# Second memory attention: keys and values made during the mix and kept in DRAM; the mix's last two products grouped around a late operand

## The chip, the cores and the metric

One Trainium2 chip, one of its cores. The core has five engines that run side by side, each with a queue of its own: PE (TensorE, matrix products into PSUM), DVE (VectorE), ACT (ScalarE), POOL (GpSimd) and SP (SyncE, which issues all the DMAs here). The metric is the time of one execution of the kernel on the device, in microseconds (us), as the median of several runs.

## The reference, cut to what matters

The program is two transformer models in a row on one sequence of 512 tokens of width 1024. The first has two layers (attention mixers, a memory attention and a feed-forward part in each). The second has one layer, and the change is in that one:

```python
p_rw, p_s5, p_gla, p_gate = split(rms_norm(x, norm_mix) @ w_in)
y_rw, y_s5, y_gla = rwkv7_mix(p_rw), s5_mix(p_s5), gla_mix(p_gla)       # 512 wide each
g = sigmoid(p_gate)                                                      # three gates, 1024 wide
x = x + (g[0]*(y_rw @ w_branch[0]) + g[1]*(y_s5 @ w_branch[1]) + g[2]*(y_gla @ w_branch[2])) @ w_out
q = rms_norm(x, norm_xattn) @ wq                                         # 4 heads of 256
k, v = split(rms_norm(mem, norm_mem) @ wkv)                              # 256 memory rows; needs no x
x = x + softmax(q @ k.T / 16) @ v @ wo
x = x + conv_ffn(rms_norm(x, norm_ffn))
```

The keys and values depend on the memory alone, which is an input. All is computed in fp32: each operand of a product is split into a high and a low half, and a product is three matmuls (high by high, high by low, low by high).

## The kernel before

Activations lie transposed, as tiles of 128 features by 512 tokens. A weight comes in from DRAM as a raw tile of 128x512 (`wraw`, 7 buffers, 256 KB); ACT copies the high half (`wh`, L312) and DVE subtracts for the low half (`wl`, L314), 5 buffers each. `proj_g` takes one block of 128 output features at a time: one PSUM bank, 8 or 4 operands deep, three matmuls each (L282 to L284), then `emit`, which takes the bank's content out. `proj_late` works on up to three chunks of 256 output features at once, with two banks for each (two of kind `mm`, two `ch`, two `si`; there are 3, 3 and 2 of them). It multiplies all operands but the last for all six banks, then asks for the last one and finishes the banks in order. In the kernel before only the first model's memory attention uses it.

The order is planned while the program is written. `kit.push` queues a generator as filler: `kind` 0 and 1 are two queues of product work that take turns, kind 2 are small steps with due times. `kit.fill(us)` runs filler for so many planned microseconds, `kit.need` runs a job to its end, and `kit.flush` runs all that is left. A scheduler then orders each engine's instructions by its own estimate of when they are ready and when a tile is free; on the chip each engine works off that list in order. Working tiles (128x512) come from rings `a`, `b`, `c`. A job's `stream` (its kind plus one, unless given) says by `kit.room` which ring it draws on: in the mix stream 0 is `a` (22 tiles), 1 is `b` (11), 2 and 3 are `c` (21).

The mix (`mix`, L2229) pushes S5 and after it GLA as kind 1; as kind 0 the low-rank part of RWKV and the gates 1 (`gates_g`, L2193). When S5 is done, merging branch 1 (`merge_g`, L2206) and gates 2 are pushed; when GLA is done, merging branch 2 and gates 0. RWKV itself (`rwkv`, L1709) runs in the foreground with fills between its steps: two pairs of `rwkv_a` steps, the inverse (`rwkv_invert`, L1487, on DVE, L1506 and L1507, while filler runs), and four `rwkv_b`, for head pairs 2, 3, 0, 1 in this order. Each `rwkv_b` ends with a norm (L468 on POOL, spread by L498 and L510), a bonus add on POOL (L1700) and a split. After that `merge_g(0)` runs: each block is multiplied by its gate on DVE (L2215), added to the sum of the other branches on POOL (L2217) and split again (L248, L245). Then `w_out` runs block by block with the memory's norm (`memory`, L2260: loads L188, splits L263 and L264, squares L2277 and adds L2278) as filler between. `add` (L1338) adds a block to x and `normed` splits it for the next products. The memory attention (`cross`, L2286) makes keys and values of head 0 and query 0, then pushes query, keys and values of heads 1 to 3 as filler for the score steps, 4.5 planned us at each.

Of the kernel before, what the change touches and what calls it, by code (L numbers as in the profile page):

```python
# [10 lines left out]
F32 = mybir.dt.float32  # L11
# [6 lines left out]
S = 512  # L18
D = 1024
DT = D // 128  # L20
MEM = 256
# [14 lines left out]
BOTH = {"mm": "mm ch si", "si": "si", "ch": "ch"}  # L36
X_BOTH = {"mm": "mm ch", "si": "si", "ch": "mm ch"}
LATE = {"mm": "mm", "si": "si", "ch": "ch", "tr": "ch"}, dict(mm=3, ch=3, si=2)
SFLOW = "accc"
AB_FILL, CD_FILL, X_FILL = (0.9, 1.2), (1.15, 1.3, 1.1), (1.1, 1.4)  # L40


# [1198 lines left out]
def layouts2(mem_2, norm_mix_2, w_in_2, rw_mu_2, rw_w0_2, rw_w_up_2, rw_a0_2, rw_a_up_2, rw_g_up_2, rw_k_k_2,  # L1241
# [20 lines left out]
    up[:16, 0] = gla_gk_up_2[0]  # L1262
    o["gk_up"] = up
    o["w_gate"] = tiled(gate)
    o["w_br"] = np.stack([tiled(z) for z in w_branch_2[0]])
    o["w_out"] = tiled(w_out_2[0])
    o["w_glu"] = tiled(s5_w_glu_2[0])
    o["mem2T"] = np.ascontiguousarray(mem_2[0].T.reshape(4, 2, 128, MEM).transpose(0, 2, 1, 3)).reshape(4, 128, 2 * MEM)
    o["xa_wq"] = tiled(xa_wq_2[0])
# [50 lines left out]
class Second:  # L1320
# [885 lines left out]
    def merge_g(self, b, ys, job):  # L2206

        kit, nc, I = self.kit, self.nc, self.I
        kit.need(job)
        sig = self.gates[b]  # L2210

        def branch(m, p):
            s = sig[m]
            if m in self.merged:
                nc.vector.tensor_tensor(s, p, s, op=ALU.mult)  # L2215
                s, z = self.merged[m], s
                nc.gpsimd.tensor_tensor(s, s, z, op=ALU.add)  # L2217
            else:
                z, s = s, kit.keep("x")
                self.merged[m] = s  # L2220
                nc.vector.tensor_tensor(s, p, z, op=ALU.mult)
            if b == 0:
                self.O.append(kit.u())
                kit.split(s, *self.O[m])

        for c in range(4):
            yield from kit.proj_g(I["w_br"][b, c], [hl for hl, _ in ys], lambda i, p: branch(2 * c + i, p))

    def mix(self):  # L2229
        kit, I = self.kit, self.I  # L2230
        self.xs = kit.xs
        self.merged, self.gates, self.O = {}, {}, []
        gla, s5 = [], []

        def branch1():
            yield from self.s5_g(s5, lambda: kit.push(branch2(), kind=1))
            kit.push(self.merge_g(1, s5, g1))
            self.g2 = kit.push(self.gates_g(2))

        def branch2():  # L2240
            yield from self.gla_g(gla)
            kit.push(self.merge_g(2, gla, self.g2))
            self.g0 = kit.push(self.gates_g(0))

        kit.push(branch1(), kind=1)
        lora = kit.push(self.rwkv_lora())
        g1 = kit.push(self.gates_g(1))
        kit.fill(20.0)
        kit.need(lora)
        rw = self.rwkv()  # L2250
        kit.flush()
        kit.run(self.merge_g(0, rw, self.g0))
        job = kit.push(self.memory(), kind=2, stream=1)
        for c in range(4):
            kit.fill(3, 10)
            kit.run(kit.proj_g(I["w_out"][c], self.O, lambda i, p: self.add(2 * c + i, p, "norm_xattn")))
        kit.need(job)


    def memory(self):  # L2260

        kit, nc, I = self.kit, self.nc, self.I
        ms = self.ms = []
        mems = [kit.load("", src=src) for src in I["mem2T"]]
        yield -6
        for m in range(DT):
            if m % 2 == 0:
                mem, hl = mems[m // 2], kit.u()
            c = slice(m % 2 * MEM, m % 2 * MEM + MEM)
            ms.append([z[:, c] for z in hl])  # L2270
            kit.split_scaled(mem[:, c], self.vec("norm_mem", m), *ms[m])
            if m == 0:
                acc = kit.f(MEM)
                nc.scalar.square(acc, mem[:, c])
            else:
                sq = kit.f(MEM)
                nc.scalar.square(sq, mem[:, c])  # L2277
                nc.gpsimd.tensor_tensor(acc, acc, sq, op=ALU.add)  # L2278
            yield -1
        self.mr = kit.t([128, 2], "mr2", 1)  # L2280
        nc.vector.tensor_copy(self.mr, kit.rpow(kit.sums(acc, kit.ones, [tok(0), tok(1)]), 1.0 / D, EPS))
        big = kit.spread_begin(self.mr, 2)
        yield -4
        self.mrb = kit.spread_end(big)

    def cross(self):  # L2286
        kit, nc, I = self.kit, self.nc, self.I
        xs, ms, mr, mrb = kit.xs, self.ms, self.mr, self.mrb
        st, O = {}, {}
        sc = kit.small(4, "scq")  # L2290

        def keys(h):
            def emit(j, p):
                if not j:
                    hl = kit.u()
                    st["k", h] = [[z[:, j * MEM : j * MEM + MEM] for z in hl] for j in range(2)]
                f = kit.f(MEM)
                nc.vector.tensor_tensor(f, p, mrb, op=ALU.mult)
                kit.split(f, *st["k", h][j])

            yield from kit.proj_g(I["xa_wk"][h], ms, emit)

        def vals(h):
            st["v", h] = []

            def emit(b, p):
                st["v", h].append(kit.u(256))
                kit.split_scaled(p, mr[:, b : b + 1], *st["v", h][b])

            yield from kit.proj_tok_g(I["xa_wv"][h], ms, [tok(0), tok(1)], emit)  # L2310

        def query(h):
            st["q", h] = []
# [37 lines left out]

            return f

        kit.run(keys(0))
        kit.run(vals(0))
        kit.run(query(0))
        jobs = [[]] + [[kit.push(g(h)) for g in (query, keys, vals)] for h in range(1, 4)]

        def heads():
            for h in range(4):  # L2360
                kit.need(*jobs[h])
                qk = []
                for (qh, ql), (kh, kl) in zip(st["q", h], st["k", h]):
                    qk += [(qh, kh), (qh, kl), (ql, kh)]
                sums = kit.small(4, "sums")
                soft = kit.soft_full(sc, [sums[:, b : b + 1] for b in range(4)])
                yield Head(kit, qk, st["v", h], [(0, 256)] * 4, DENSE_K[:2], soft, done(h, sums), 4.5)

        kit.attention(heads())
        kit.flush()  # L2370
# [95 lines left out]
def program(tc, ctx, I, out):  # L2466
    kit = Kit(tc, ctx, I)
    f = First(kit)
    kit.banks(*APART)
    kit.room("abbb", a=26, b=31)  # L2470
    V, P = kit.nc.vector, kit.nc.gpsimd
    f.begin()
    kit.by(P)
    f.mixer_ab()
    kit.by(V)
    kit.share(X_BOTH)
    f.cross(0)
    kit.share(BOTH)
    kit.room("aaaa", a=50)
    f.ffn(0, f.g_mix[1])  # L2480
    kit.share(APART[0])
    kit.by(V, P)
    kit.room("abbb", a=24, b=33)
    f.mixer_cd()
    kit.by(V)
    kit.share(X_BOTH)
    f.cross(1)
    kit.banks(*LATE)
    kit.room("abbb", a=31, b=50-31)
    s = Second(kit)  # L2490
    take, done = handover(kit, f, s)
    job = kit.push(s.s5_make_g())
    f.ffn(1, take)
    kit.need(job)
    done()
    kit.room("abcc", a=22, b=11, c=54-22-11)
    s.reset = kit.load("reset")
    s.mix()
    kit.flow(SFLOW)
    s.cross()  # L2500
    kit.room("aaaa", a=50)
    s.ffn()
    s.finish(out)
# [13 lines left out]
```

## Time and profile before

| | before |
|---|---|
| median of 3 runs | 2703.43 us (2700.62 to 2705.85) |
| the profiled execution | 2697.67 us |
| its span, first to last instruction | 2695.9 us |
| PE busy | 2573.7 us (95%) |
| DVE busy | 1594.7 us (59%) |
| ACT busy | 1180.1 us (44%) |
| POOL busy | 518.9 us (19%) |
| DMA | 258.51 MB, 96 GB/s on the mean |
| granted TensorE clock, mean | 0.978 of full speed |

The mix of the second model runs from about 1441 us to 2153 us of the span (its last output products overlap with the keys of head 0), the memory attention until about 2327. Busy shares are of the whole span; what a stage is bound by has to be read in that stage. PE's matmuls overlap, so the durations printed for them are longer than the distance of their starts.

### The profile page before, as it was taken

The numbers are of one execution on the slowest core, as the hardware profiler recorded it, in microseconds if no ns is written. First come the engines' busy times: TensorE is split into PE (matmuls) and PEld (weight loads), VectorE is DVE, ScalarE is ACT, GpSimd is POOL, SyncE is SP. The second block draws the span as 40 slices with busy tenths as digits, with TensorE's granted clock in tenths as the row PEclk, the third lists the DMA queues.
The fourth block names the chain that finished last, engine by engine and source line by source line (L and its number), as shares of the span: only waits on it lengthen the run. The fifth ranks groups of instructions, "written<-read, shape, count | busy, mean of one in ns | idle before, by whom it ended". The sixth has DMA issues, their size and how long they took to land. (4 is left out here: it accounts for less than half of the span.)

```text
span 2695.9 us, 37069 instructions
## 1 busy us (share of the span) xinstructions
PE 2573.7 (95%) x13432; PEld 2083.8 (77%) x13432; DVE 1594.7 (59%) x3076; ACT 1180.1 (44%) x2208; POOL 518.9 (19%) x439
## 2 busy tenths in 40 slices
PE   8999999999999999999999989799999999999998
PEld 6668778888776787787877767587777798888886
DVE  5686654344457876876335477654464656774673
ACT  5576543233445765332334322435233445543443
POOL 5325021010211131143103232112231300100001
PEclk9999999999999999999999989899999999999999
DMA  4112223333322131334433553421222333233332
GB/s 155 36 51 87 67 85 93 101 97 93 116 89 71 44 98 47 114 118 145 126 106 110 167 170 98 102 97 60 71 79 70 119 119 97 83 97 95 98 94 70
DMA packets 172520, 258.51 MB, mean 96 GB/s; under 512 B 42528, under 2 KB 60832, under 8 KB 172320
## 3 DMA queue, kind: packets, MB, share of 16 engines
q1 hardware_dynamic: 172336, 256.13, 31.2%
q8 instruction: 106, 1.74, 0.3%
q14 instruction: 78, 0.64, 0.1%
HBM read 234.04 MB, written 22.15 MB: 95 GB/s over the span
## 5 line engine op out<-in xcount | busy, mean ns | idle before, releaser
L312 ACT CAST wh<-wraw 128x512 fp32r<-128x512 f32 (+1 forms) x777 | 473.3, 613 | 886.4 <-PE ps_mm L283 606.9
L314 DVE TENSOR_TENSOR wl<-wraw,wh 128x512 fp32r<-128x512 f32 (+1 forms) x691 | 491.7, 715 | 355.5 <-ACT wh L312 343.5
L284 PE MATMUL ps_mm<-xs,wl 128*128 128x512 f32 x1544 | 612.6, 397 | 22.4 <-DVE wl L314 21.5
L282 PE MATMUL ps_mm<-xs,wh 128*128 128x512 f32 x1544 | 623.2, 404 | 9.0 <-ACT wh L312 8.3
L283 PE MATMUL ps_mm<-xs,wh 128*128 128x512 f32 x1544 | 612.6, 397 | 3.0 <-DVE xs L264 2.9
L284 PEld LDWEIGHTS ps_mm<-xs,wl 128*128 128x128 f32 x1544 | 293.8, 190 | 89.6 <-DVE wl L314 24.1
L282 PEld LDWEIGHTS ps_mm<-xs,wh 128*128 128x128 f32 x1544 | 294.1, 190 | 76.4 <-ACT wh L312 8.7
L283 PEld LDWEIGHTS ps_mm<-xs,wh 128*128 128x128 f32 x1544 | 293.6, 190 | 66.2 <-DVE xs L264 6.4
L448 POOL TENSOR_TENSOR acc<-acc,za 128x512 f32<-128x512 f32 x59 | 82.0, 1391 | 729.5 <-ACT za L444 728.2
L282 PE MATMUL ps_mm<-za,wh 128*128 128x512 f32 x460 | 183.2, 398 | 5.6 <-ACT za L248 5.6
L284 PE MATMUL ps_mm<-za,wl 128*128 128x512 f32 x460 | 182.3, 396 | 4.1 <-DVE wl L314 4.1
L283 PE MATMUL ps_mm<-za,wh 128*128 128x512 f32 x460 | 180.7, 393 | 0.2 <-DVE za L245 0.2
L314 POOL TENSOR_TENSOR wl<-wraw,wh 128x512 fp32r<-128x512 f32 x86 | 112.5, 1316 | 304.9 <-ACT wh L312 300.1
L1193 POOL TENSOR_TENSOR za<-za,za 128x512 f32<-128x512 f32 x44 | 60.0, 1364 | 462.0 <-ACT za L1192 462.0
L284 PEld LDWEIGHTS ps_mm<-za,wl 128*128 128x128 f32 x460 | 87.5, 190 | 24.5 <-DVE wl L314 4.5
L282 PEld LDWEIGHTS ps_mm<-za,wh 128*128 128x128 f32 x460 | 87.6, 190 | 24.3 <-ACT za L248 6.4
L282 PE MATMUL ps_mm<-zb,wh 128*128 128x512 f32 (+1 forms) x284 | 100.4, 354 | 4.4 <-ACT zb L248 4.4
L283 PEld LDWEIGHTS ps_mm<-za,wh 128*128 128x128 f32 x460 | 87.3, 190 | 20.5 <-DVE za L245 1.0
L245 DVE TENSOR_TENSOR za<-ps_tr,za 128x512 fp32r<-128x512 f32 (+3 forms) x152 | 84.6, 558 | 31.2 <-ACT za L248 29.9
L283 PE MATMUL ps_mm<-zb,wh 128*128 128x512 f32 (+1 forms) x284 | 97.4, 344 | 0.1
L284 PE MATMUL ps_mm<-zb,wl 128*128 128x512 f32 (+1 forms) x284 | 97.3, 343 | 0.0
L468 POOL TENSOR_TENSOR rs<-sm,neghalf 128x4 f32<-128x4 f32 (+2 forms) x32 | 45.3, 1416 | 240.3 <-DVE sm L467 240.3
(590 smaller groups left out, 4768.2 us busy)
## 6 DMA issues: line engine op xcount, KB each, us to landing
wraw<-w_gu SPq DMA_DIRECT2D x176, 256.0 KB, 2.7
wraw<-w_dn SPq DMA_DIRECT2D x96, 256.0 KB, 2.6
wraw<-w_up SPq DMA_DIRECT2D x88, 256.0 KB, 2.6
wraw<-w_gate SPq DMA_DIRECT2D x48, 256.0 KB, 2.8
wraw<-w_dn SPq DMA_DIRECT2D x48, 192.0 KB, 2.3
dram<-za SPq DMA_DIRECT2D x26, 256.0 KB, 2.5
zc<-dram SPq DMA_DIRECT2D x26, 256.0 KB, 4.5
wraw<-w_cd SPq DMA_DIRECT2D x24, 256.0 KB, 2.7
```

The source lines that it names most:

```text
L245: self.nc.vector.tensor_tensor(lo, src, hi.bitcast(F32), op=ALU.subtract)
L282: mm(out, ah, bh, start=start, stop=False, **kw)
L283: mm(out, ah, bl, start=False, stop=False, **kw)
L284: mm(out, al, bh, start=False, stop=stop, **kw)
L312: self.nc.scalar.copy(hl[0], raw)
L314: eng.tensor_tensor(hl[1], raw, hl[0].bitcast(F32), op=ALU.subtract)
L448: self.nc.gpsimd.tensor_tensor(self.acc[0], self.acc[0], sq, op=ALU.add)
L468: self.nc.gpsimd.tensor_tensor(r, ms, self.neghalf[:, :n], op=ALU.pow)
L1193: nc.gpsimd.tensor_tensor(a, a, st["rb"], op=ALU.mult)
```

## The change

- `w_br0` (branch 0's weights) and `w_out` are laid out in chunks of 256 columns, and `merge_g(0)` and the product with `w_out` go through `proj_late`. The late operand is the last of the list: `ys[-1]`, head pair 3, and `self.O[-1]`.
- `memory` is pushed at the start of the mix (kind 2), loads its input piece by piece, and behind it `memory_kv` is queued as kind 0, ahead of gates 1. It makes keys and values of all four heads and stores them, high and low halves, in a DRAM scratch of 16 tiles. A store is issued when the first block of the next product is taken out.
- After `merge_g(0)` the 16 tiles are loaded back into ring `b`. `cross` no longer makes keys and values; its fill is 2.7 instead of 4.5.
- In the mix ring `b` has 18 tiles instead of 11; the map of streams to rings for the end is `acbc` instead of `accc`, and is set in `mix`.

```diff
-SFLOW = "accc"
+SFLOW = "acbc"
+C_FILL = 2.7
...
-    o["w_br"] = np.stack([tiled(z) for z in w_branch_2[0]])
-    o["w_out"] = tiled(w_out_2[0])
+    o["w_br0"] = chunked(w_branch_2[0][0], 256)
+    o["w_br"] = np.stack([tiled(z) for z in w_branch_2[0][1:]])
+    o["w_out"] = chunked(w_out_2[0], 256)
...
+        if b == 0:
+            emit = lambda c: lambda i, p: branch(2 * c + i, p)
+            kit.proj_late([(I["w_br0"][c], [hl for hl, _ in ys[:-1]], emit(c)) for c in range(4)], lambda: ys[-1][0])
+            return
         for c in range(4):
-            yield from kit.proj_g(I["w_br"][b, c], [hl for hl, _ in ys], lambda i, p: branch(2 * c + i, p))
+            yield from kit.proj_g(I["w_br"][b - 1, c], [hl for hl, _ in ys], lambda i, p: branch(2 * c + i, p))
...
         lora = kit.push(self.rwkv_lora())
+        kit.push(self.memory_kv(kit.push(self.memory(), kind=2, stream=1)))
         g1 = kit.push(self.gates_g(1))
...
         kit.run(self.merge_g(0, rw, self.g0))
-        job = kit.push(self.memory(), kind=2, stream=1)
-        for c in range(4):
-            kit.fill(3, 10)
-            kit.run(kit.proj_g(I["w_out"][c], self.O, lambda i, p: self.add(2 * c + i, p, "norm_xattn")))
-        kit.need(job)
+        kit.flow(SFLOW)
+        self.kv = []
+        for h in range(4):
+            self.kv.append([kit.r(stream=2) for _ in range(4)])
+            for z, d in zip(self.kv[h], self.kv_dram[h]):
+                kit.nc.sync.dma_start(z.bitcast(F32), d)
+        emit = lambda c: lambda i, p: self.add(2 * c + i, p, "norm_xattn")
+        kit.proj_late([(I["w_out"][c], self.O[:-1], emit(c)) for c in range(4)], lambda: self.O[-1])
...
+    def memory_kv(self, job):
+        kit, nc, I = self.kit, self.nc, self.I
+        self.kv_dram = self.scratch([4, 4, 128, S])
+        kit.need(job)
+        late = []
+        def store():
+            for z, d in late:
+                nc.sync.dma_start(d, z.bitcast(F32))
+            late.clear()
+        def keys(h):
+            hl = []
+            def emit(j, p):
+                if not j:
+                    hl[:] = kit.u()
+                c = slice(j * MEM, j * MEM + MEM)
+                f = kit.f(MEM)
+                nc.vector.tensor_tensor(f, p, self.mrb, op=ALU.mult)
+                kit.split(f, *(z[:, c] for z in hl))
+                if j:
+                    late.extend((z, self.kv_dram[h, i]) for i, z in enumerate(hl))
+                else:
+                    store()
+            return kit.proj_g(I["xa_wk"][h], self.ms, emit)
...
+        for h in range(4):
+            yield from keys(h)
+            yield from vals(h)
+        yield -3
+        store()
...
-        kit.run(keys(0))
-        kit.run(vals(0))
         kit.run(query(0))
-        jobs = [[]] + [[kit.push(g(h)) for g in (query, keys, vals)] for h in range(1, 4)]
+        jobs = [[]] + [[kit.push(query(h))] for h in range(1, 4)]
...
-                yield Head(kit, qk, st["v", h], [(0, 256)] * 4, DENSE_K[:2], soft, done(h, sums), 4.5)
+                yield Head(kit, qk, st["v", h], [(0, 256)] * 4, DENSE_K[:2], soft, done(h, sums), C_FILL)
...
-    kit.room("abcc", a=22, b=11, c=54-22-11)
+    kit.room("abcc", a=22, b=18, c=21)
     s.reset = kit.load("reset")
     s.mix()
-    kit.flow(SFLOW)
     s.cross()
```

## Rows read from the trace of the kernel before

**Rows 1.** Busy time by stage: us, length, busy of each engine, clock, DMA, GB/s

```profile
1441.00:2064.00 623.00, 573.32 (x3717) 464.36 (x3715) 361.51 (x680) 224.41 (x381) 148.01 (x119) 0.96 0.34 104
2064.00:2116.00 52.00, 39.58 (x181) 30.20 (x180) 32.97 (x47) 20.79 (x41) 20.86 (x17) 0.84 0.37 112
2116.00:2327.00 211.00, 210.40 (x1192) 182.05 (x1190) 121.45 (x221) 104.38 (x196) 19.96 (x15) 1.00 0.33 101
```

**Rows 2.** Timeline around the hole: start, us, instruction, idle before it and its releaser

```profile
1681.65 0.68 DVE L2199 TENSOR_TENSOR zb<-ps_mm,acc 128x512 f32<-128x512 f32 x1
...
1703.03 0.79 PE L284 MATMUL ps_mm<-xs,wl 128*128 128x512 f32 x1 [14.58 <-DVE wl L314]
```

**Rows 3.** Busy time, inverse stretch and the stretch ahead of it

```profile
1661.00:1703.00 42.00, 27.45 (x226) 20.21 (x222) 36.62 (x105) 4.00 (x7) 7.75 (x5) 0.88 0.43 104
...
1590.00:1660.00 70.00, 62.82 (x387) 49.91 (x384) 48.97 (x78) 29.21 (x45) 23.10 (x16) 0.90 0.49 150
```

**Rows 4.** DVE's groups by line, 1661 to 1703: count, busy us, mean ns, idle

```profile
L1507 DVE TENSOR_TENSOR zc<-zc,zc 128x14 f32<-128x14 f32 (+35 forms) x44 | 13.2, 301 | 1.3
```

**Rows 5.** Timeline of PE in the tail of the mix

```profile
2069.36 1.05 PE L460 MATMUL ps_ch<-half,za 128*128 128x2 f32 x8 [0.69 <-ACT za L1691]
2072.95 1.09 PE L510 MATMUL ps_ch<-ident,za 128*128 128x128 f32 x4 [2.54 <-DVE za L498]
...
2078.74 1.65 PE L282 MATMUL ps_mm<-zc,wh 128*128 128x512 f32 x3 [3.42 <-ACT zc L248]
...
2080.61 0.63 PE L284 MATMUL ps_mm<-zc,wl 128*128 128x512 f32 x1
2081.04 0.63 PE L282 MATMUL ps_mm<-zc,wh 128*128 128x512 f32 x1
...
2082.06 0.39 PE L282 MATMUL ps_mm<-zc,wh 128*128 128x512 f32 x1
...
2107.09 0.50 PE L282 MATMUL ps_mm<-za,wh 128*128 128x512 f32 x1 [2.57 <-ACT za L248]
...
2111.53 0.79 PE L282 MATMUL ps_mm<-za,wh 128*128 128x512 f32 x1 [2.98 <-ACT za L248]
```

**Rows 6.** PE's groups by shape in the attention, 2120 to 2330: count, busy us

```profile
L282 PE MATMUL ps_mm<-wh,zb 128*128 128x256 f32 x64 | 18.1, 283 | 0.0
```

**Rows 7.** Timeline of PE: two key matmuls, 18 starts apart

```profile
2249.24 0.28 PE L282 MATMUL ps_mm<-zb,wh 128*128 128x256 f32 x1
...
2251.36 0.28 PE L282 MATMUL ps_mm<-zb,wh 128*128 128x256 f32 x1
```

**Rows 8.** DVE's groups by shape in the attention, 2120 to 2265: mean ns

```profile
L314 DVE TENSOR_TENSOR wl<-wraw,wh 128x512 fp32r<-128x512 f32 x61 | 42.4, 696 | 35.2 <-ACT wh L312 35.0
...
L264 DVE SCALAR_TENSOR_TENSOR zc<-ps_mm,mr,zc 128x256 fp32r<-128x256 f32 x6 | 2.9, 480 | 2.2 <-ACT zc L263 1.7 <-PE ps_si L283 0.5
...
L2298 DVE TENSOR_TENSOR zc<-ps_mm,zb 128x256 f32<-128x256 f32 x6 | 2.5, 424 | 0.3
```

**Rows 9.** POOL's groups, 2074 to 2116

```profile
L2217 POOL TENSOR_TENSOR x<-x,zb 128x512 f32<-128x512 f32 x8 | 12.4, 1549 | 12.8 <-DVE zb L2215 12.7
```

**Rows 10.** Line 264, 2060 to 2120: duration ns min/median/max, first and last start

```profile
L264 DVE SCALAR_TENSOR_TENSOR zb<-zb,vecs,zb x8: 472/970/1517, 2090.8 to 2111.0; 128x256 fp32r<-128x256 f32 x8
```

**Rows 11.** DMA issues, 1441 to 2330: KB each, median us to landing

```profile
dram<-za SPq DMA_DIRECT2D x26, 256.0 KB, 2.5
zc<-dram SPq DMA_DIRECT2D x26, 256.0 KB, 4.5
```

**Rows 12.** SP's own waits, 1441 to 2330: us in total, times, longest

```profile
SPq L2099 <- ACT zc L2164: 17.0, 2, 12.0
...
SPq L1465 <- DVE za L1435: 11.8, 2, 11.2
...
SPq L188 <- POOL x L2217: 9.6, 1, 9.6
```

**Rows 13.** Busy time, the first model's second memory attention

```profile
940.00:1030.00 90.00, 89.89 (x539) 77.99 (x538) 61.49 (x113) 56.65 (x112) 22.38 (x17) 1.00 0.31 92
```

More of the change, by code (lines that the diff above doesn't have):

```diff
@@ L2263, in memory @@
         ms = self.ms = []
-        mems = [kit.load("", src=src) for src in I["mem2T"]]
-        yield -6
         for m in range(DT):
             if m % 2 == 0:
-                mem, hl = mems[m // 2], kit.u()
+                mem, hl = kit.load("", src=I["mem2T"][m // 2]), kit.u()
+                yield -4
             c = slice(m % 2 * MEM, m % 2 * MEM + MEM)
@@ L2284, in memory, with vals, emit @@
         self.mrb = kit.spread_end(big)
+    def memory_kv(self, job):
[21 more added lines that the diff above has]
+            return kit.proj_g(I["xa_wk"][h], self.ms, emit)
+        def vals(h):
+            hl = []
+            def emit(b, p):
+                if not b:
+                    hl[:] = kit.u()
+                c = slice(b * 256, b * 256 + 256)
+                kit.split_scaled(p, self.mr[:, b : b + 1], *(z[:, c] for z in hl))
+                if b:
+                    late.extend((z, self.kv_dram[h, 2 + i]) for i, z in enumerate(hl))
+                else:
+                    store()
+            return kit.proj_tok_g(I["xa_wv"][h], self.ms, [tok(0), tok(1)], emit)
+        for h in range(4):
+            yield from keys(h)
+            yield from vals(h)
+        yield -3
+        store()
@@ L2286, in cross @@
     def cross(self):
         kit, nc, I = self.kit, self.nc, self.I
-        xs, ms, mr, mrb = kit.xs, self.ms, self.mr, self.mrb
+        xs = kit.xs
         st, O = {}, {}
         sc = kit.small(4, "scq")
[L2292 to L2310, printed above, removed]
+        for h, (kh, kl, vh, vl) in enumerate(self.kv):
+            st["k", h], st["v", h] = ([[z[:, j * MEM : j * MEM + MEM] for z in hl] for j in range(2)] for hl in ((kh, kl), (vh, vl)))
         def query(h):
```

## The prediction

> **What bounds the kernel now.** I read the page first: TensorE (PE) is busy 95% of the 2695.9 us span and no other engine above 59%. So only two things can shorten the run: less PE work, or less time in which PE stands idle or runs slowly. The change removes no matmul. It moves some, so the question is where PE idles now. The table of stages answers it [rows 1]: the mix before its last products (1441 to 2064) has 573 busy of 623 us, the tail of the mix (2064 to 2116) 39.6 of 52 at a granted clock of 0.84, the second memory attention (2116 to 2327) 210.4 of 211 at clock 1.00. The last is full; the first two have room.
>
> The longest single idle time of PE in the mix is a hole of 14.58 us that ends at 1703, at the low half of a projection's weight, which VectorE (DVE) splits [rows 2]. In that stretch DVE is busy 36.6 of 42 us while PE has 27.5 [rows 3], because DVE works through the rows of the inverse: 44 products of one kind alone take 13.2 us [rows 4]. The first gates had their last product out of PSUM near 1682 [rows 2], and the next job of that queue, merging branch 1, waits for the S5 branch. The filler queue `kind=0` was empty just where it was wanted.
>
> The second place is the tail [rows 5]. After nine matmuls of the merge (k=0 of three banks) PE waits 0.69, 2.54 and 3.42 us for the last RWKV head pair's norm, bonus and split, and later 2.57 and 2.98 us for the last two operands of the output product: 12.2 us. After each wait it restarts slowly: matmuls of 0.63 us where they take 0.39 once the clock is back. Slow ones start 0.43 us apart, quick ones 0.24 (twice the 0.118 us of a 256-column matmul, below); I count some 22 slow ones, 0.2 us each: 4.4 us. In all 16.6 us.
>
> **The change part by part.**
>
> *Keys and values made in the mix.* 384 matmuls of 256 columns leave the attention in six groups of 64, of which one stands [rows 6], at 0.118 us apart (18 steps in 2.12 us) [rows 7]: 45.3 us of PE work. With them go, on DVE, 32 weight splits of 0.70 us, for each of eight key blocks two steps of 0.42 us (the norm's factor, and a low half of the same size), and eight value steps of 0.48 us [rows 8]: 32.8 us. The job is queued ahead of the first gates, so all later filler shifts back by 45 us. By itself this is worth nothing: PE does the same work elsewhere. It gains what idle time it covers.
>
> *The hole at 1703.* With the keys and values ahead, the first gates (192 matmuls of 512 columns, about 45 us) start one such job later and still run when the S5 branch is awaited. The hole is then 14.6 us of idle plus some six slow matmuls (1.2 us), 15.8 us to win. DVE limits it: gates cost 16 splits of 0.70 and 8 steps of 0.68 per 45 us, 0.37 us of DVE per us of PE, so 14.6 us want 5.4, and 42 - 36.6 = 5.4 are free. It just fits. Bounds 0 (DVE keeps the inverse in front) to 15.8; I take 12, near the upper end, since the space is there.
>
> *The tail.* 45 us minus some 15 used in the hole leave about 30 us of the last gates after the final RWKV step. They can stand where PE now waits 6.65 us, and when they end the merge has all operands. Here the grouped merge itself does little: its late operand is the last in the list, head pair 3, while the loop finishes the pairs in the order 2, 3, 0, 1. Without leftover filler, 18 matmuls instead of 9 could run ahead, 2.1 us more. In the output product the grouping fits: operands 0 to 6 of three column chunks are 126 matmuls (29 us) before the last is asked for. But six merge banks now end together, and their eight adds on GpSimd (POOL) take 1.55 us each [rows 9], 12.4 us, against some 5.5 us of remaining merge work; the first output products want one operand per 1.4 us, so 0 to 6 us can show. Memory's norm, whose POOL and DVE steps stood between those adds, is gone from there. I take 3 us left of 16.6: gain 13.6.
>
> *Early mix.* From 1590 to 1660 DVE has 49 of 70 us [rows 3]. There the keys and values stand in for gates, at 32.8 / 45.3 = 0.72 us of DVE per us of PE instead of 0.37; for a whole job of 45 us that is 15 us more, 64 of 70. It fits on average, not at each moment: loss 0 to 10, taken 4.
>
> On memory's norm itself: its eight low-half steps, with two inputs in SBUF, took 0.47 to 1.52 us (median 0.97) beside POOL's adds [rows 10], against 0.48 us for a like step that reads PSUM [rows 8]. The Trainium skill, "SBUF — State Buffer", section "Who interferes with whom", says that a DVE instruction with two SBUF inputs and a GpSimd instruction that reads SBUF lock each other out for a whole instruction. The trace agrees. By that rule the early mix, where POOL works too, would pay about 8 x 0.5 = 4 us of DVE, which speaks against moving it there, and it would make the 64 of 70 us 68.
>
> *Stores and reloads.* 16 stores and 16 loads of 256 KB. Stores of that size landed in 2.5 us, loads in 4.5 [rows 11]. A store is issued one product block after its data, so SyncE (SP) should not stand at it; cost 0, hidden by weights loaded ahead (up to seven). The reloads need 16 of 18 `b` tiles while the gates hold eight, so the last six wait for merge evictions, and output weights queue behind them on SP. In the present tail one memory load stood 9.6 us on SP until a POOL add freed its tile [rows 12]. Cost 0 to 10; taken inside the 3 us above, since several output weights are loaded by then.
>
> *The attention.* It loses 45 us of cover out of 211. What is left per score step is 2.7 us of filler. The first model's second attention has as thin a fill, and PE there is busy 89.9 of 90 us [rows 13]. The start is new: the first query needs all eight normed columns at once, where 11 us of keys and values stood between. Loss 0 to 6, taken 2.
>
> **Sum.** 12 + 13.6 - 4 - 2 = 19.6 us. The profiled execution took 2697.67 us (span 2695.9), the median of the runs is 2703.43, 5.8 us above; shifted by that: 2697.7 - 19.6 + 5.8 = 2683.9, say 2684.
>
> **The rivals.**
> 1. *Both holes close fully* and no new wait appears: 15.8 + 16.6 = 32.4 us, 2671. For it: DVE's free 5.4 us and full cover in the like attention. Against: a queue in order rarely packs so well. 0.17.
> 2. *One hole only*: the inverse still runs in front of the splits, or the early mix eats all that the leftover brings. 13.6 - 4 - 2, or 12 - 6 + 2 (the 18 early matmuls): some 8 us, 2696. For it: DVE at 36.6 of 42. 0.15.
> 3. *The change doesn't do what it says*: filler is not left over at the end, and the merge's late operand is not the late one, so the waits only move: 2703. For it: the loop's order. 0.10.
> 4. *Slower: the stores stand on SP and the `b` tiles run out.* In the early mix 18 `b` tiles hold eight of memory, four of keys and values, four of the low-rank halves, the spread norm and one scratch tile: exactly all. A store stuck on SP behind another wait holds its tiles, the next head's products can't be taken out of PSUM, and three banks are soon full. Two groups of moves in this stretch kept SP waiting 17.0 and 11.8 us, up to 12.0 at once [rows 12]. If PE stood for all of it, 28.8 us take the place of the 4: 2684 + 24.8 = 2709. Against: 28.8 us of SP's waiting lie mostly where no store is due, and S5 and RWKV work could go on. It decides from some 25 us of PE waiting there. 0.08.
>
> **How the numbers follow.** Forecast 2684 (2676 to 2692) 0.50; rivals 0.17, 0.15, 0.10, 0.08. The range 2664 to 2703 leaves out rival 4, part of 3, and gains beyond 39 us. Within 0.2% (5.4 us, about what a measurement of this kernel can tell from no change) lie rival 3 and a little of 2: same 0.13, slower 0.08, faster 0.79.
>
> **What would show it.** Right: no PE idle above 3 us in the inverse stretch; gates still running when the last head pair's norm waits; no wait at the last two output operands; attention some 45 us shorter. Wrong: L314 still behind the inverse; DVE near full from 1590 to 1660 with PE waiting for it; SP waiting in front of the stores or, for POOL, in front of output weights; PE waiting at scores or at the first query.

## The result, and the profile after

The changed kernel takes 2720.32 us (median of 4 runs, 2719.49 to 2721.82) against 2703.89 for the kernel before beside it: 1.0062 times as long [1.0049, 1.0075], 16 us slower where 20 us faster was forecast. The profiled execution's span is 2718.9 us (2695.9 before). The page of after:

```profile
span 2718.9 us, 37112 instructions
PE 2595.7 (95%) x13432; PEld 2097.8 (77%) x13432; DVE 1596.8 (59%) x3076; ACT 1176.4 (43%) x2206; POOL 520.7 (19%) x439
PEclk9999999999998999999999987899999999999999
```

The same 13432 PE instructions keep PE busy 22 us longer: the work is equal, PE did it more slowly. Where, the stages of after show (columns as in [rows 1]; the early mix, the inverse, the S5 branch's end, the RWKV steps, the tail with both grouped products, the attention):

```profile
1590.00:1660.00 70.00, 59.01 (x437) 53.69 (x437) 51.54 (x83) 25.37 (x45) 23.01 (x17) 0.81 0.56 184
1660.00:1755.00 95.00, 75.19 (x482) 61.60 (x483) 64.24 (x152) 29.43 (x52) 13.11 (x8) 0.84 0.55 157
1755.00:1820.00 65.00, 56.97 (x246) 38.43 (x245) 32.28 (x46) 22.68 (x38) 5.45 (x4) 0.95 0.29 81
1820.00:2138.00 318.00, 306.62 (x2342) 254.46 (x2341) 159.59 (x309) 124.09 (x217) 68.89 (x61) 0.98 0.24 75
2138.00:2192.00 54.00, 49.90 (x209) 40.50 (x208) 25.96 (x35) 16.39 (x27) 11.96 (x8) 0.94 0.63 199
2192.00:2350.00 158.00, 156.79 (x762) 129.02 (x760) 93.05 (x162) 76.68 (x146) 20.46 (x14) 1.00 0.24 76
```

The tail is better (clock 0.94 with 50 of 54 us busy; [rows 1] had 0.84 with 39.6 of 52), the attention full. The three lines from 1590 to 1820 are the loss: clock 0.81, 0.84, and in the third only 246 products in 65 us. The same 230 us in one line, of before and then of after:

```profile
1590.00:1820.00 230.00, 202.41 (x1379) 162.24 (x1376) 150.84 (x297) 87.43 (x146) 49.35 (x38) 0.93 0.41 119
```

```profile
1590.00:1820.00 230.00, 191.16 (x1161) 153.73 (x1160) 148.06 (x280) 77.48 (x133) 41.57 (x29) 0.86 0.48 144
```

Less work done, a lower clock, and no engine near full apart from PE: DVE has 148 of 230 us.

To compare kernels whose order differs, I sum PE's need: every matmul's columns (one with fewer than 128 is counted as 128) at 0.461 ns, which is the 0.118 us per 256 of [rows 7]. What a stretch takes beyond the need is its excess. It splits into idle time (the waits that the timeline shows), half of the time in which PE worked at the lower of its two clock levels (1.2 instead of 2.4 GHz), and a rest. Each trace is counted from the first low-rank weight load of the mix (1441.1 before, 1442.9 after); "early" is 149 to 379 us from there (1590 to 1820), "late" from there to the first load of the feed-forward part. In us, one execution each:

| kernel | early excess | idle | half clock | late excess |
|---|---|---|---|---|
| before | 50.7 | 27.6 | 10.2 | 53.6 |
| after | 83.3 | 38.8 | 27.3 | 42.7 |
| e1 no low halves of key/value weights | 62.2 | 25.9 | 16.7 | 37.8 |
| e2 whole block per turn | 69.2 | 41.2 | 15.9 | 40.9 |
| e3 keys and values last | 52.3 | 29.3 | 8.9 | 54.3 |
| e4 all but keys and values | 70.2 | 27.4 | 28.3 | 50.2 |
| e6 4 of 16 stores | 76.6 | 36.3 | 23.1 | 41.4 |
| e7 six weight tiles | 62.1 | 31.6 | 17.0 | 37.0 |
| e8 no grouping | 82.8 | 39.0 | 27.1 | 42.9 |
| e9 before, six weight tiles | 51.1 | 27.9 | 9.2 | 55.9 |
| e10 before, early norm | 71.2 | 27.4 | 28.3 | 49.7 |
| e11 six tiles, whole blocks | 66.1 | 38.5 | 15.0 | 40.1 |
| e14 before, norm 60 us later | 51.8 | 29.2 | 8.4 | 53.4 |
| e16 values side by side | 66.7 | 33.3 | 16.4 | 42.7 |
| e18 six tiles, norm later | 59.9 | 29.6 | 14.6 | 35.7 |

The change won 10.9 us late and lost 32.6 early: 11.2 more idle, 17.1 by the clock, 4.3 rest. That is a net loss of 21.7 us where the medians differ by 16, because the traced execution of before was 5.8 us quicker than its median.

**How the early loss looks.** From 1755 to 1820, groups of ACT and PE (line, engine, operation, tiles, count | busy, mean ns | idle before, and who ended it):

```profile
L283 PE MATMUL ps_mm<-xs,wh 128*128 128x512 f32 x38 | 16.9, 444 | 4.1 <-ACT wh L313 4.0
L313 ACT CAST wh<-wraw 128x512 fp32r<-128x512 f32 x13 | 8.0, 617 | 26.5 <-PE ps_mm L284 26.5
L283 PE MATMUL ps_mm<-wh,xs 128*128 128x256 f32 x9 | 2.7, 304 | 0.0
```

and single casts and products of that stretch (start, duration, [idle before <- releaser]):

```profile
1774.09 0.62 ACT L313 CAST wh<-wraw 128x512 fp32r<-128x512 f32 x1 [3.16 <-PE ps_mm L284]
1778.04 0.62 ACT L313 CAST wh<-wraw 128x512 fp32r<-128x512 f32 x1 [2.36 <-PE ps_mm L284]
1774.76 0.50 PE L283 MATMUL ps_mm<-zc,wh 128*128 128x512 f32 x1 [0.47 <-ACT wh L313]
1778.71 0.50 PE L283 MATMUL ps_mm<-xs,wh 128*128 128x512 f32 x1 [0.48 <-ACT wh L313]
```

ACT waits for PE to leave a weight tile, casts the next weight into it, and PE waits for that cast: only one tile of the five changes hands. The other four belong to GLA's value product over tokens (`ps_mm<-wh,xs`, `proj_tok_g`), which asks for all its weights at once, keeps them over its token blocks, and gives the turn to the other queue after each operand. Before, the gates 1 were finished when it came, and its first half ran almost by itself (32 of each of its three products from 1710 to 1740); now the gates 1, pushed back by the keys and values, take turns with it for a hundred us. The values of the new job are such a product too.

The hole of [rows 2] has given way to another. Before, PE waited for a low half that DVE made behind the inverse; now the casts for the last values stand on ACT behind GLA's decay steps:

```profile
1715.21 0.69 ACT L1757 ACTIVATE zc<-ps_si,vecs 128x512 f32<-128x512 f32 x1 [1.03 <-PE ps_si L285]
1716.65 0.63 ACT L1759 ACTIVATE zc<-zc 128x512 f32<-128x512 f32 x1 [0.76 <-DVE zc L1758]
1717.30 1.28 ACT L1760 ACT_TABLE_LOAD   x1
1718.59 0.63 ACT L1760 ACTIVATE zc<-zc 128x512 f32<-128x512 f32 x1
1719.24 1.28 ACT L1767 ACT_TABLE_LOAD   x1
1721.40 0.63 ACT L1767 ACTIVATE zc<-zc 128x512 f32<-128x512 f32 x1 [0.87 <-DVE zc L1762]
1722.04 2.16 ACT L313 CAST wh<-wraw 128x512 fp32r<-128x512 f32 x4
```

```profile
1713.00 0.28 PE L285 MATMUL ps_mm<-zb,wl 128*128 128x256 f32 x1
1722.69 0.79 PE L283 MATMUL ps_mm<-wh,zb 128*128 128x256 f32 x2 [7.58 <-ACT wh L313]
```

The keys' last product freed its tile at 1713.0, but four casts run together only at 1722.0. That freer tiles would have put them ahead of the decay in ACT's queue is not shown: with a sixth tile PE still waits 7.47 us for such a group of four casts (e7), and where the values' weights are used up one at a time no cast costs PE more than 1.9 us at once (e16).

### The profile page after: what moved, and what is told of

It reads as the page before. It is cut to its first block, busy times and chain, and to the rows that moved or that the text cites. A ratio compares the mean times of both kernels' runs of the same rounds, so it can differ in the third digit from the quotient of the medians.

```text
span 2718.9 us, 37112 instructions
## 1 busy us (share of the span) xinstructions
PE 2595.7 (95%) x13432; PEld 2097.8 (77%) x13432; DVE 1596.8 (59%) x3076; ACT 1176.4 (43%) x2206; POOL 520.7 (19%) x439
## 3 DMA queue, kind: packets, MB, share of 16 engines
q1 hardware_dynamic: 176944, 264.52, 31.6%
## 5 line engine op out<-in xcount | busy, mean ns | idle before, releaser
L284 PEld LDWEIGHTS ps_mm<-xs,wh 128*128 128x128 f32 x1544 | 294.4, 191 | 66.1 <-DVE xs L265 6.0
L283 PE MATMUL ps_mm<-za,wh 128*128 128x512 f32 x428 | 170.6, 399 | 4.1 <-DVE zb L2217 4.1
L285 PE MATMUL ps_mm<-za,wl 128*128 128x512 f32 x428 | 169.1, 395 | 4.1 <-DVE wl L315 4.1
L284 PE MATMUL ps_mm<-za,wh 128*128 128x512 f32 x428 | 168.0, 393 | 0.0
L285 PEld LDWEIGHTS ps_mm<-za,wl 128*128 128x128 f32 x428 | 81.3, 190 | 23.5 <-DVE wl L315 4.5
L283 PEld LDWEIGHTS ps_mm<-za,wh 128*128 128x128 f32 x428 | 81.4, 190 | 21.0 <-DVE zb L2217 4.5
L284 PEld LDWEIGHTS ps_mm<-za,wh 128*128 128x128 f32 x428 | 81.3, 190 | 17.9
```

Of the source, the lines that this page charges most:

```text
L283: mm(out, ah, bh, start=start, stop=False, **kw)
L284: mm(out, ah, bl, start=False, stop=False, **kw)
L285: mm(out, al, bh, start=False, stop=stop, **kw)
```

## The experiments

Two theories to begin with: A, the weight tiles; B, DVE's time (my own term for the early mix). C is the prediction's rival 4, the stores. Times are medians; ratios are against the kernel before on the same chip, for which the changed kernel's is 1.0062 [1.0049, 1.0075].

**e1, no low halves of the new weights** (`highs` is set while keys and values are advanced; cut to `load_split`).

```diff
-        hl = [z[:, :n] for z in hl or [self.t([128, CW], t, NW, F32R) for t in ("wh", "wl")]]
+        hl = [z[:, :n] for z in hl or [self.t([128, CW], t, NW, F32R) for t in (("wh",) if self.highs else ("wh", "wl"))]]
         self.nc.scalar.copy(hl[0], raw)
+        if self.highs:
+            return [hl[0], hl[0]]
         eng = next(self.halves)
```

> The changed kernel, but the weights of the keys and values get no low half of their own: the high half is used twice, so the 32 subtractions on DVE (0.70 us each, 22 us) between 1590 and 1740 are left out, while PE's products, ACT's casts, loads and stores stay. Theory A (weight buffers: a product over tokens holds four of the five weight tiles, its casts stand in a line behind the last readers): the casts on ACT and their buffers are as before, so little changes, 2714 to 2721. Rival B (DVE: keys and values want 0.72 us of DVE per us of PE beside the inverse): the excess of PE's time over its need from 1590 to 1755, 62 us against 44 in the kernel before, goes back by 15 to 18, 2702 to 2706.

2698.51 us, 0.9985 [0.9973, 0.9997]: 22 us back, below A's range and past B's too, so it speaks for B if taken alone. But the edit does more than leave out DVE's steps: the new job no longer takes low-half tiles either, so those are left to the other products.

**e2, whole blocks per turn.**

```diff
-                yield m1 * 1.3e-3
+            yield len(xs) * m1 * 1.3e-3
```

> The changed kernel, but a product over tokens gives the turn to the other queue after a whole block of eight operands instead of after each operand, so it holds its four weight tiles for a shorter time. Theory A: the stretch from 1755 to 1820, where every weight of the gates is cast only after the one before it was read (PE 45 us of need in 65 us), closes up, 10 to 15 us less there, and some of 1590 to 1755: 2702 to 2710. Rival B (DVE) and rival C (stores on SP): no difference, 2716 to 2722.

2704.83 us, 1.0003 [0.9992, 1.0014]: 15 us back, which B has no place for. The stretch that A named closes in part (322 products where after has 246; first line). But early idle time did not fall (41.2 against 38.8): with most casts in time, PE stands 13.16 us for a low half that DVE makes behind the inverse, the hole of [rows 2] again (second line). What fell most is the time at half clock, from 27.3 to 15.9 us.

```profile
1755.00:1820.00 65.00, 60.02 (x322) 48.93 (x321) 39.74 (x55) 37.89 (x62) 12.71 (x10) 0.97 0.34 99
1697.33 0.58 PE L285 MATMUL ps_mm<-zb,wl 128*128 128x256 f32 x1 [13.16 <-DVE wl L315]
```

**e5, the low halves of these weights on POOL** (`split_by`), asks whether e1 won by DVE's time.

```diff
-        eng = next(self.halves)
+        eng = next(self.halves) if self.split_by is None else next(self.split_by)
```

> The changed kernel, but the low halves of the keys' and values' weights are subtracted on POOL instead of DVE (32 subtractions; POOL is busy 23 of 70 us from 1590 to 1660 where DVE has 49 before and more after). Leaving those 32 steps out gave 22 us. If it is DVE's time that they cost, moving them gives most of that: 2700 to 2708. If it is the step itself (POOL takes 1.2 to 1.5 us where DVE takes 0.70, and each weight is used up in 1.4 us of PE), or if POOL and DVE hinder each other, little or nothing is won: 2714 to 2728.

2726.25 us, 1.0071 [1.0053, 1.0089]: nothing won. The step got longer (first POOL in e5, then DVE in after, both 1590 to 1760):

```profile
L326 POOL TENSOR_TENSOR wl<-wraw,wh 128x512 fp32r<-128x512 f32 x32 | 43.6, 1385 | 50.3 <-ACT wh L324 50.2
```

```profile
L315 DVE TENSOR_TENSOR wl<-wraw,wh 128x512 fp32r<-128x512 f32 (+1 forms) x46 | 35.6, 793 | 12.5 <-ACT wh L313 12.5
```

DVE's time was freed and did not help, though the step itself also got longer; and DVE was at 148 of 230 us in after. So B falls as a matter of DVE's busy time. What e1 took away besides is a link of the chain load, cast, subtraction, product, and the new job's hold on low-half tiles; how its 22 us divide between these no run separates. DVE's order is another matter: e2 shows it.

**e7, a sixth weight tile, and e9, the same in the kernel before** (there without the second edit).

```diff
-NW = 5
+NW = 6
...
-    kit.room("abcc", a=22, b=18, c=21)
+    kit.room("abcc", a=22, b=18, c=19)
```

> The changed kernel with six weight tiles of each half instead of five (ring c has 19 tiles instead of 21 for it), so that beside a product over tokens, which holds four, the gates have two. Theory A: the series of cast and product from 1755 to 1820 opens up as it did with whole blocks per turn (15 us): 2703 to 2711. If the casts were late for another reason (ACT's order, DVE): 2715 to 2722.

> The kernel before with six weight tiles of each half instead of five, nothing else. The sixth tile gave 24 us in the changed kernel. If that came from the products over tokens that the change puts beside other projections (theory A), the kernel before, where these products run by themselves or in the attention, gains little: 2698 to 2706. If a sixth tile helps everywhere (the hole at 1703, the tail), 2680 to 2694.

e7: 2695.82 us, 0.9965 [0.9948, 0.9982], 24 us less than the changed kernel and more than A's own range gave it. e9: 2707.72 us, 1.0020 [1.0010, 1.0031], nothing won. So the sixth tile is worth nothing in the kernel before, which has neither token products beside other projections nor the early norm.

**e16, values side by side.** Both token blocks get a PSUM bank each, and the loop runs over weight tiles outside, so a tile is free after its own twelve matmuls. (Of the edit, the call alone; `side` is that loop.)

```diff
-            return kit.proj_tok_g(I["xa_wv"][h], self.ms, [tok(0), tok(1)], emit)
+            return side(I["xa_wv"][h], emit)
```

> The changed kernel with five weight tiles and the same turns, but the value products of the keys-and-values job take both token blocks side by side in two PSUM banks, so that a weight tile is freed after its own twelve matmuls instead of being held for both blocks. GLA's token products hold their four tiles as before. If the tiles held by the values made the loss from 1600 to 1700: 2700 to 2710, and no 15 us of lag between 1640 and 1690. If the loss there is the clock's or the norm's: 2715 to 2722.

2706.98 us, 1.0011 [1.0000, 1.0021], 13 us less than the changed kernel at five tiles. With e7 (first) the same three stretches as above, then e16's, whose trace begins the mix 3.5 us later:

```profile
1755.00:1820.00 65.00, 64.42 (x354) 52.37 (x353) 31.88 (x48) 26.20 (x48) 7.79 (x7) 1.00 0.30 80
1660.00:1755.00 95.00, 73.88 (x435) 62.34 (x434) 63.31 (x152) 32.75 (x57) 11.86 (x8) 0.82 0.59 168
1590.00:1660.00 70.00, 60.13 (x521) 54.07 (x521) 53.44 (x94) 25.72 (x48) 23.57 (x17) 0.88 0.60 193
```

```profile
1590.00:1660.00 70.00, 58.47 (x483) 53.41 (x482) 51.77 (x87) 26.49 (x46) 24.65 (x17) 0.88 0.61 197
1660.00:1755.00 95.00, 75.17 (x455) 60.91 (x456) 65.35 (x155) 34.32 (x58) 9.44 (x6) 0.87 0.57 163
1755.00:1820.00 65.00, 63.16 (x316) 48.27 (x314) 35.80 (x50) 27.34 (x48) 10.95 (x8) 1.00 0.33 90
```

From 1755 to 1820 PE is full again at full clock: 354 and 316 products instead of 246. PE's waits for a cast, 1590 to 1820, in after, e7, e2 and e16 (us in total, times, longest):

```profile
PE ps_mm L283 <- ACT wh L313: 19.8, 13, 7.6
PE ps_mm L283 <- ACT wh L313: 16.3, 5, 7.5
PE ps_mm L283 <- ACT wh L313: 5.2, 3, 2.6
PE ps_mm L283 <- ACT wh L313: 4.5, 3, 1.9
```

That is theory A for the series of casts, by three edits that share nothing but the tiles: one more of them, held shorter, held by one job less. It is not A alone for the whole 13 to 24 us: of the early excess that these edits gave back (21.2, 14.1 and 16.6 us in e7, e2 and e16), 10 to 11 us in each is time at half clock, and whether the tiles or merely another order of the instructions brought that back, these runs don't say.

**e6, 4 of 16 stores** (all reloads read head 0's tiles).

```diff
             for z, d in late:
-                nc.sync.dma_start(d, z.bitcast(F32))
+                if self.stored < 4:
+                    nc.sync.dma_start(d, z.bitcast(F32))
+                self.stored += 1
```

> The changed kernel, but only head 0's four tiles of keys and values are stored; the other 12 stores are left out, and all 16 reloads read head 0's tiles. Rival C of the prediction (stores stand on SP and hold the b tiles): they would give back what they cost, 2695 to 2710. If SP's short waits at the stores (16 us in all, up to 6.1 at once) hide beside other work: 2716 to 2722.

2714.07 us, 1.0029 [1.0016, 1.0043]: some 6 us, between both expectations. The stores cost something, and it is small. That they cost it by standing on SP is not shown. SP's queue in after, 1590 to 1820 (waited for: us in total, times, longest; the stores are L2304, and their longest single wait was 4.7 us, not the 6.1 of the expectation):

```profile
SPq L311 <- DVE wl L315: 71.5, 31, 7.0
SPq L2304 <- ACT zb L264: 6.1, 2, 4.2
SPq L2304 <- DVE zb L265: 4.7, 1, 4.7
```

**e8, no grouping:** `merge_g(0)` and `w_out` block by block as before.

> The changed kernel, but the last two products of the mix go block by block as before, without groups; keys and values stay in the mix. The tail then has the leftover gates but no grouping. If the leftover gates alone close the waits of 12 us (the prediction's account of the tail), 2718 to 2724, the same as the changed kernel. If the grouping carries the tail, 2728 to 2736. If the grouping costs something, 2708 to 2715.

2723.90 us (2720.37 to 2728.52), 1.0068 [1.0051, 1.0085]; late excess 42.9 against 42.7. The leftover gates alone make the tail's gain; the grouping adds nothing that can be told.

**e3, keys and values behind gates 0; e4, all of the change but the keys and values** (the last line below is e3's alone).

```diff
-        kit.push(self.memory_kv(kit.push(self.memory(), kind=2, stream=1)))
+        mem = kit.push(self.memory(), kind=2, stream=1)
...
+            kit.push(self.memory_kv(mem), stream=2)
```

> The changed kernel, but keys and values are queued behind the last gates (gates 0), with their working tiles from ring c; the memory's norm stays early. If the place is what costs (A or B: beside the inverse, S5 and the GLA products), the early mix runs as in the kernel before with its hole of 14.6 us, and 45 us of filler cover the tail: 2703 less 10 to 14, that is 2689 to 2694. If keys and values cost wherever they are made in the mix (stores and reloads, two weights per product time), 2705 to 2720.

> The changed kernel, but keys and values are made in the attention as before (no stores, no reloads, 4.5 planned us of filler per score step, map of rings accc); the grouped last products and the early memory norm stay. If the grouping is worth little by itself, 2698 to 2704, with the tail of the mix still waiting some 10 us. If the grouping or the early norm carries the loss, 2712 to 2722.

e3: 2709.06 us, 1.0010 [0.9997, 1.0023], in the range for a cost wherever they are made. Its trace says otherwise: the early loss is gone (52.3 against 50.7 in before), so the place did cost. The gain of the tail is missing because late, where idle time fell from 24.5 to 17.8 us, the time at half clock rose from 8.3 to 18.1. e4: 2716.00 us, 1.0045 [1.0030, 1.0060]. e4 was the surprise: no keys and values in the mix, and still slower, with early idle time as in before and 28.3 us by half clock. One part was left that I had costed at nothing worth the name.

**e10, the early norm alone, in the kernel before; e14, the same begun 60 planned us later (on the chip its steps ran 20 to 35 us later); e13, only a shift.** The first line below is in e10 and e14, at the start of the mix instead of after `merge_g(0)`, with ring `b` and the loading piece by piece as in the changed kernel; the second, as the first statement of `memory`, in e14; the third, eight times and alone, in e13.

```diff
+        kit.push(self.memory(), kind=2, stream=1)
...
+        yield -60
...
+            kit.nc.tensor.matmul(p, z[:, :128], z, start=True, stop=True)
```

> The kernel before, but the memory's norm is made at the start of the mix as in the changed kernel (ring b with 18 tiles for it); keys and values, the last products and the attention as before. The version with the grouped last products and the early norm took 2716. If the early norm carries that (its DVE, ACT and POOL steps beside the early mix, or a lower clock there), 2711 to 2718. If it is the grouping without leftover filler, 2699 to 2706.

> The kernel before with the memory's norm early, but begun 60 planned us later in the mix. If the norm's own steps beside the early mix cost the clock, the loss stays in part, 2708 to 2718. If it was the few places at the start of the mix where its steps came before others on DVE and ACT, 2700 to 2706.

> The kernel before with eight products more (512 columns, 0.24 us each, 1.9 us) at the start of the second model's mix, whose result nobody reads. If the clock in the early mix hangs on when each stretch begins, the time moves by more than these 2 us: 2710 to 2720, or under 2698. If not, 2703 to 2708.

e10: 2719.10 us, 1.0062 [1.0044, 1.0080], as much as the whole change. e14: 2705.55, 1.0008 [0.9996, 1.0021]. e13: 2702.91, 1.0000 [0.9986, 1.0014]. In e10's trace the loss is the clock alone: idle 27.4 as before, 28.3 us by half clock against 10.2; e4 has the same 27.4 and 28.3. In windows of 10 us, e10 first, then e3, whose queues on PE, DVE, ACT and POOL hold the same instructions in the same order up to about 2000 us, at the same point of the mix:

```profile
1644.00:1654.00 10.00, 10.00 (x64) 8.85 (x60) 3.89 (x13) 0.00 (x0) 0.00 (x0) 0.50 0.30 102
1654.00:1664.00 10.00, 10.00 (x34) 7.56 (x34) 6.17 (x12) 1.88 (x4) 0.00 (x0) 0.55 0.36 79
```

```profile
1648.00:1658.00 10.00, 9.55 (x54) 7.43 (x55) 9.73 (x25) 2.15 (x4) 0.00 (x0) 1.00 0.53 168
1658.00:1668.00 10.00, 10.00 (x54) 7.35 (x54) 5.54 (x12) 3.34 (x7) 0.00 (x0) 1.00 0.43 81
```

PE has no idle time in e10's windows and works at half clock all the same; e3's stands at full clock and does the 93 products of e10's 20 us in 13. The waits of PE just ahead are the same in both: 1.61, 1.79 and 1.36 us in e10, 1.62, 1.80 and 1.36 in e3. Behind the last of them the clock was low for 30.7 us in e10 and for 3.4 in e3. So in these two traces neither the order of the instructions, nor idle time in the stretch, nor the waits just ahead tell which level is granted. It is no stray of one execution: e4, another kernel on another chip, has such a stretch of 30.7 us at the same point of the mix (first line), and after has one of 20 (second line).

```profile
1628.40:1659.10 30.70, 29.66 (x132) 23.03 (x133) 21.82 (x40) 4.82 (x10) 6.52 (x6) 0.50 0.24 72
1646.70:1667.00 20.30, 20.30 (x127) 16.32 (x126) 9.61 (x26) 3.57 (x7) 0.00 (x0) 0.50 0.36 110
```

That DVE is not the way the norm costs is seen too: e10 has it busy 138 of 230 us, before 151.

**e11, e12, e15, e17, e18, what adds up.** Below is the order's edit; the others stand above. Six tiles with whole blocks per turn (e11); that with head pair 1 as the merge's late operand (e12); six tiles with that order (e15); the same with values side by side (e17); six tiles with the norm later (e18).

```diff
-    o["w_br0"] = chunked(w_branch_2[0][0], 256)
+    o["w_br0"] = chunked(w_branch_2[0][0].reshape(4, 128, D)[[2, 3, 0, 1]].reshape(4 * 128, D), 256)
...
+            ys = [ys[t] for t in (2, 3, 0, 1)]
```

> The changed kernel with six weight tiles (ring c 19) and with whole blocks per turn in products over tokens. Alone they gave 24 and 15 us. If both relieve the same shortage of weight tiles, together they give hardly more than the better one: 2690 to 2698. If they are different losses, 2678 to 2686.

> As the version with six weight tiles and whole blocks per turn, but the merge's grouped product takes head pair 1, which the loop finishes last, as its late operand instead of pair 3. If the merge waits for that pair, 1 to 4 us less than that version. If the leftover gates cover it in any order, the same within 2 us.

> The changed kernel with six weight tiles (ring c 19) and head pair 1 as the merge's late operand, products over tokens taking turns after each operand as before. If the order is worth its 6 us here too: 2688 to 2692, clearly under the kernel before. If not: 2693 to 2698, as with six tiles alone.

> As the version with the value products side by side, with six weight tiles (ring c 19) and head pair 1 as the merge's late operand. If side by side and the sixth tile relieve different jobs (values, GLA's token products): 2685 to 2692. If the sixth tile already did both: 2693 to 2700.

> The changed kernel with six weight tiles, and the memory's norm begun up to 60 planned us later (just before the keys and values need it). If the norm's place at the start of the mix and the weight tiles are two losses that add, 2680 to 2688. If the sixth tile already removed what both cost, or the norm's loss there hung on the order of just that kernel, 2693 to 2700.

| kernel | us | ratio to before |
|---|---|---|
| e11 | 2705.69 | 1.0007 [0.9997, 1.0017] |
| e12 | 2699.47 | 0.9987 [0.9977, 0.9998] |
| e15 | 2698.71 | 0.9980 [0.9972, 0.9989] |
| e17 | 2703.97 | 1.0002 [0.9993, 1.0011] |
| e18 | 2698.37 | 0.9967 [0.9953, 0.9982] |

Nothing adds to the sixth tile, and two remedies together were worse than the better one: e11 and e17 missed both of their expectations. In e11 the hole of [rows 2] is back, 15.5 us behind DVE's low half, as in e2; for e17 I have no reason. The late operand's order gave 6 us in e12 and none in e15. Of the six versions with six tiles, e7, e15 and e18 are 0.2% to 0.35% quicker than the kernel before, e12 hardly, e11 and e17 not. In e7 that is the tail's gain, with the early loss cut to a third.

## Why the prediction was wrong, point by point

- **The tail: right.** Forecast 13.6 gained there and 2 lost in the attention, 11.6; the late excess fell by 10.9. Gates still ran when the last head pair's norm was awaited. One wait is left at the start of `w_out`, for the gate step on DVE that empties one of the merge's PSUM banks, in place of 12.2 us of waits before; I had left 3:

```profile
2174.16 0.79 PE L283 MATMUL ps_mm<-za,wh 128*128 128x512 f32 x1 [4.10 <-DVE zb L2217]
```

- **The grouping: right** that it does little with leftover filler (e8).
- **Moved PE work and the attention: right.** 156.8 of 158 us busy at clock 1.00 with 2.7 us of filler.
- **The hole at 1703: the step that failed.** I asked whether DVE had 5.4 us to spare and took 12 us gained. DVE's free time was not what decides. In the changed kernel the longest wait there is 7.58 us for casts that stand on ACT behind GLA's decay steps; and where whole blocks per turn bring the casts in time (e2, e11), the keys' low half stands behind the inverse on DVE after all, for 13.16 and 15.5 us, one of the signs that I had named for being wrong. The 5.4 us were free on DVE, but not ahead of the inverse. Idle time early rose by 11.2 us instead of falling.
- **The early mix: the second that failed, by what it counted.** I forecast DVE at 64 of 70 us and a loss of 4, at most 10; DVE had 51.5 of 70 (49 before), and the early excess grew by 32.6 us where hole and early mix together were to win 8. I summed DVE's time per us of PE and never counted weight tiles: five of them, four taken by one product over tokens. Of the 32.6 us, 11.2 are idle time and 17.1 the clock, a term that the sum took as given. I had listed five tiles of each half for the kernel and used the number nowhere; rival 4 even counted the `b` tiles and left the weight tiles out.
- **What a queue shift meets.** I noted that all later filler shifts by 45 us, and wrote that by itself this is worth nothing. It is what set the gates 1 beside GLA's value product.
- **Memory's norm: priced at some 4 us of DVE by a rule, and at nothing in the sum.** Alone it cost 16 us, all of it clock (e10), and nothing when begun later (e14). The rule of the Trainium skill, "SBUF — State Buffer", section "Who interferes with whom", was not what bound here: the eight low-half steps took 4.6 us in all at the new place, less than eight of the median of 0.97 that [rows 10] had, which would be 7.8.
- **Rival 4: right side, wrong mechanism.** It named a slower time of 2709 with PE waiting in the early mix, at 0.08. Leaving out 12 of its 16 stores gave back some 6 us (e6); the rest of the loss is elsewhere.
- **The profiled execution.** Before's was 5.8 us quicker than its median, and I shifted by that. In 126 runs of that kernel on five chips the time falls by 2.3 us for each 0.001 that the mean clock is higher (2710.7 us at 0.973, 2697.8 at 0.978, in two of them): the shift was the clock, which my sum took as given.

Not settled: why the norm near the start of the mix goes with a lower clock 130 us later in e10 and e4, and not in e3, which has the same instructions there (each a single trace); the shift by 1.9 us (e13) changed nothing. Nor is it shown how much of the changed kernel's 17 us of clock comes from the norm and how much from the waits for weight tiles, since the clock rose with each edit that shortened those waits (27.3 to 16 or 17 in e1, e2, e7 and e16), and the norm later gave nothing on top of six tiles (e18). Two runs that would separate them were not made: the changed kernel at five tiles with the norm later, and the kernel before with the early norm and a sixth tile.

## What to carry to other kernels

Before moving work into a stretch with room, list every pool that the moved job draws on (weight tiles, PSUM banks, rings) and what the job that it pushes aside will meet: a product that holds four of five buffers while it takes turns with another puts that other one on a chain of load, cast, split and product. Where such a pool decides, hold each buffer for a shorter time or add one, and use a control without the change to see that the gain belongs to it. And an average over an engine's busy time says nothing of order: the casts here waited on an engine that was a third busy.

## What the runs showed of the hardware that was not expected

- PE without any idle time worked 20 us at half clock (e10, 1644 to 1664), where the same 93 products took 13 us at full clock in another trace (e3), behind the same waits. Such a stretch came in e4 and in the changed kernel too. With some thirty small steps of DVE, ACT and POOL 130 us ahead of it, e10 took 16 us longer than the kernel before; e3's trace has the same steps and no such loss there.
- The mean clock accounts for most of the spread between runs of one kernel: 2.3 us per 0.001, with a correlation of -0.91, over 126 runs of the kernel before from 2697.5 to 2717.3.
- The subtraction that took DVE 0.79 us on the mean in the changed kernel took POOL 1.39 us in e5.
